# Differential attention: issuing the score matmuls of the two components in turn, each into its own bank

## The chip, the cores and the metric

The kernel runs as one program on one core of one Trainium2 chip. The metric is the device time of one execution in microseconds (us): 2513.7 us is the median of three runs of the kernel before (2513.29 to 2515.72). The engines go by their short names: PE is TensorE, DVE VectorE, ACT ScalarE, POOL GpSimd, SP SyncE with the DMA queue that it issues.

## The reference, cut to what matters

The program is two transformer blocks in float32 on 512 tokens of width 1024: a state space branch and a mixture of experts, then a recurrent layer (RWKV-7) and a layer of differential attention. The change lies in that attention, the last layer, where each of 8 heads has two components (c) of 64 dimensions:

```python
def block(args):                       # 128 queries at a time
    q_blk, blk = args
    s = jnp.einsum('bhcqd,bhckd->bhcqk', q_blk.astype(f32), kf)
    q_pos = blk * Q_BLOCK + jnp.arange(Q_BLOCK)
    s = jnp.where(k_pos[None, :] <= q_pos[:, None], s, -1e30)
    prob = jax.nn.softmax(s, axis=-1)
    attn = prob[:, :, 0] - lam * prob[:, :, 1]
    return jnp.einsum('bhqk,bhkv->bhqv', attn, vf)
```

The result is normalized over the 128 values of a head, multiplied by `silu(gate)` and projected.

## The kernel before, in words

A float32 product is made of three matmuls of a rounded kind (float32r): each operand is split into a high and a low part, and high by high, high by low and low by high are added up in one PSUM bank. `mm3` (L199 to L206) does it for the projections (L205), `hilo` (L222 to L224) splits: the high part on ACT (L223), the low part on DVE or POOL (L224).

`LayerB.run` (L2376) goes through 32 units, one for each head `m` and block of 128 queries `i`, for the heads 0 to 5 in the order i = 0, 1, 2, 3. A unit of block `i` has `n = 128 (i + 1)` keys, since the mask is causal. `unit` (L2280) is a generator of three steps:

- Step one, the score maps. For each component c, three matmuls at L2297 (64 partitions of k and q: 0 to 63 for c = 0, 64 to 127 for c = 1) fill a map of 128 x n in a PSUM tile `sm`. DVE adds the mask to its last 128 columns (L2298) and takes the maximum (L2299), ACT exponentiates with the sum of each row (L2300). Then DVE puts the two components together into one map `e0` (L2302 to L2304; L2304 is the large one).
- Step two. PE transposes `e0` block by block (L2309) into another `sm`, ACT copies it to `aT` (L2311), PE multiplies by the values into the bank `o` (L2313). ACT squares and sums (L2316), DVE (L2317) and POOL (L2318) make the factor, ACT writes the scaled `ot` (L2319).
- Step three, for odd `i`: PE transposes the `ot` of the two latest blocks into an `sm` (L2326), DVE multiplies by the gate into `y` (L2328), which is then split.

The tag `sm` has three PSUM banks (L2287), shared by all of this. A round of `run` takes step three of the unit before the last, step two of the last and step one of the new one.

Between the units stand steps of `head_in` (L2223), which projects k, q and gate of the next head: 24 matmuls at L205 for each of six groups, on PE alone. For k and q the partly rotated positions follow: ACT copies the result to `rp` (L2243), SP moves four bands of it to `turn` by DMA (L2246), POOL multiplies `rp` (L2248) and DVE multiplies `turn` (L2249) by tables of cosines and sines, DVE adds (L2250) and the sum is split into `hdkh`, `hdkl` or `hdqh`, `hdql`.

The order of instructions on each engine isn't that of the code. The program is recorded under a tile framework with `schedule_with_timeline_sim=True`: it keeps the data's dependences and picks the order by a timeline of its own, and `issue_after` (L2232) holds back the projections' matmuls until the marked score matmul of an earlier unit (`self.marks`, L2301). At run time each engine goes through its list in that order and waits at semaphores.

Of the kernel before, what the change touches and what calls it, by code (L numbers as in the profile page):

```python
# [1571 lines left out]
class Pre:  # L1572
# [25 lines left out]
    def t(self, n, b=1, w=512, dt=F32):  # L1598
        return self.sp.tile([P, w], dt, tag="p_" + n, name="p_" + n, bufs=b)
# [543 lines left out]
class LayerB:  # L2143
# [136 lines left out]
    def unit(self, m, i, hd, o, yo):  # L2280

        g, nc = self.g, self.g.nc
        t = lambda shape, name, bufs=2: self.sp.tile(shape, F32, tag=name, name=name, bufs=bufs)
        sm = lambda: g.ps.tile([P, 512], F32, tag="sm", name="sm", bufs=3)  # L2287
        kr, qr = hd["k"], hd["q"]
        n = (i + 1) * P
        qs = slice(i * P, n)  # L2290
        r, mx = t([P, 6], "sums", 4), t([P, 2], "mx")
        e = [t([P, 512], "e%d" % c) for c in range(2)]
        for c in range(2):
            f = slice(64 * c, 64 * c + 64)
            p = sm()
            for j, (a_, b_) in enumerate(((qr[0], kr[0]), (qr[0], kr[1]), (qr[1], kr[0]))):
                mark = nc.tensor.matmul(p[:, :n], lhsT=a_[f, qs], rhs=b_[f, :n], start=j == 0, stop=j == 2).ins  # L2297
            nc.vector.tensor_add(p[:, qs], p[:, qs], self.cst[:, 1024:])  # L2298
            nc.vector.tensor_reduce(mx[:, c:c + 1], p[:, :n], axis=AX.X, op=OP.max, negate=True)  # L2299
            nc.scalar.activation(e[c][:, :n], p[:, :n], AF.Exp, bias=mx[:, c:c + 1], accum_out=r[:, c:c + 1])  # L2300
        self.marks.append(mark)  # L2301
        nc.vector.reciprocal(r[:, 2:3], r[:, 1:2])  # L2302
        nc.vector.scalar_tensor_tensor(r[:, 2:3], r[:, 2:3], self.nlam, r[:, 0:1], op0=OP.mult, op1=OP.mult)
        nc.vector.scalar_tensor_tensor(e[0][:, :n], e[1][:, :n], r[:, 2:3], e[0][:, :n], op0=OP.mult, op1=OP.add)  # L2304
        nc.vector.scalar_tensor_tensor(r[:, 3:4], r[:, 0:1], 1e-5, r[:, 0:1], op0=OP.mult, op1=OP.mult)
        yield 1
        p = sm()
        for j in range(i + 1):
            nc.tensor.transpose(p[:, j * P:(j + 1) * P], e[0][:, j * P:(j + 1) * P], g.ident)  # L2309
        aT = t([P, 512], "aT")  # L2310
        nc.scalar.activation(aT[:, :n], p[:, :n], AF.Copy)  # L2311
        for j in range(i + 1):
            nc.tensor.matmul(o[:, qs], lhsT=aT[:, j * P:(j + 1) * P], rhs=self.vt[:, j, m * P:(m + 1) * P],  # L2313
                             start=j == 0, stop=j == i)
        ot = t([P, P], "ot", 4)
        nc.scalar.activation(ot, o[:, qs], AF.Square, accum_out=r[:, 4:5])  # L2316
        nc.vector.scalar_tensor_tensor(r[:, 4:5], r[:, 4:5], 1.0 / 128, r[:, 3:4], op0=OP.mult, op1=OP.add)  # L2317
        nc.gpsimd.tensor_tensor(r[:, 5:6], r[:, 4:5], g.mhalf[:, 0:1], op=OP.pow)  # L2318
        nc.scalar.activation(ot, o[:, qs], AF.Copy, scale=r[:, 5:6])  # L2319
        yield 1  # L2320
        th, d = divmod(i, 2)
        hd["o", i] = ot
        if d:
            p = sm()
            for c in range(2):
                nc.tensor.transpose(p[:, c * P:(c + 1) * P], hd["o", i - 1 + c], g.ident)  # L2326
            y = t([P, 256], "y")
            nc.vector.scalar_tensor_tensor(y, p[:, :256], self.sl, hd["g"][:, 256 * th:256 * th + 256], op0=OP.mult,  # L2328
                                           op1=OP.mult)
            g.hilo(yo[th][0][:, m], yo[th][1][:, m], y)  # L2330
# [141 lines left out]
```

## Time and profile before

| | |
|---|---|
| median of three runs | 2513.7 us |
| the profiled execution's own time | 2504.29 us |
| its span, first to last instruction | 2502.5 us |
| PE, DVE, ACT, POOL busy | 91%, 52%, 35%, 31% of the span |
| units of attention, first score map to the last unit's | 2173.5 to 2418 us of the span |

The time of a row in the timeline is counted from the start of the span. A matmul's end is modelled: one of 256 columns is shown with 0.28 us while the next starts 0.12 us after it, so what PE takes is read from starts. In the timeline equal instructions that follow each other in time stand in one row with their count (x2). "[1.16 <-DVE e L2304]" behind a row is the engine's idle time before it and what ended it. PEclk is the granted clock of TensorE: 1.00 is 2.4 GHz and 0.50 is 1.2 GHz.

### The profile page before, as it was taken

The numbers are of one execution on the slowest core, as the hardware profiler recorded it, in microseconds if no ns is written. First come the engines' busy times: TensorE is split into PE (matmuls) and PEld (weight loads), VectorE is DVE, ScalarE is ACT, GpSimd is POOL, SyncE is SP. The second block draws the span as 40 slices with busy tenths as digits, with TensorE's granted clock in tenths as the row PEclk, the third lists the DMA queues.
The fourth block names the chain that finished last, engine by engine and source line by source line (L and its number), as shares of the span: only waits on it lengthen the run. The fifth ranks groups of instructions, "written<-read, shape, count | busy, mean of one in ns | idle before, by whom it ended". The sixth has DMA issues, their size and how long they took to land. (4 is left out here: it accounts for less than half of the span.)

```text
span 2502.5 us, 31640 instructions
## 1 busy us (share of the span) xinstructions
PE 2283.3 (91%) x11912; PEld 1641.4 (66%) x11912; DVE 1308.8 (52%) x2382; ACT 876.6 (35%) x1597; POOL 771.3 (31%) x596
## 2 busy tenths in 40 slices
PE   6899999998998999999989976998979899999997
PEld 3677888776886544443334335666868798988887
DVE  5567877767643433211111126758525556477765
ACT  3443333343322211111111115535326644354552
POOL 2333434114001122222212224449324221655212
PEclk9899999999999999999999987999979999999998
DMA  7232333344733889999999963576765432122211
GB/s 287 94 101 101 103 108 108 119 145 159 268 101 119 338 302 399 381 347 387 399 382 362 376 203 117 152 187 189 205 175 200 144 105 88 56 60 65 79 65 51
DMA packets 187178, 477.16 MB, mean 191 GB/s; under 512 B 62333, under 2 KB 111869, under 8 KB 146832
## 3 DMA queue, kind: packets, MB, share of 16 engines
q1 hardware_dynamic: 161392, 424.48, 47.1%
q0 software_dynamic: 16288, 37.21, 5.7%
q10 hardware_dynamic: 9344, 13.44, 1.8%
q8 instruction: 94, 1.54, 0.2%
q14 instruction: 60, 0.49, 0.1%
HBM read 423.66 MB, written 71.89 MB: 198 GB/s over the span
## 5 line engine op out<-in xcount | busy, mean ns | idle before, releaser
L224 POOL TENSOR_TENSOR wl<-wr,wh 128x1024 fp32r<-128x1024 f32 x80 | 202.9, 2553 | 373.2 <-ACT wh L223 373.2
L223 ACT ACTIVATE wh<-wr 128x1024 fp32r<-128x1024 f32 (+1 forms) x202 | 204.3, 1043 | 236.1 <-PE mm L205 147.7
L205 PE MATMUL mm<-uh,wh 128*128 128x512 f32 x640 | 258.4, 404 | 10.4 <-DVE cv L604 7.6
L205 PE MATMUL mm<-ul,wh 128*128 128x512 f32 x640 | 256.1, 400 | 0.0
L205 PE MATMUL mm<-uh,wl 128*128 128x512 f32 x640 | 255.7, 400 | 0.0
L1196 PE MATMUL mm<-m_we,m_x 128*64 128x512 f32 (+1 forms) x672 | 250.7, 599 | 0.3 <-DMA m_we<-in_w_exp_dram 0.3
L205 PE MATMUL mm<-ya,wh 128*128 128x256 f32 x1280 | 243.9, 291 | 6.8 <-ACT wh L223 6.7
L205 PEld LDWEIGHTS mm<-ya,wh 128*128 128x128 f32 x1280 | 204.9, 196 | 13.9 <-ACT wh L223 7.9
L224 DVE TENSOR_TENSOR wl<-wr,wh 128x1024 fp32r<-128x1024 f32 (+1 forms) x122 | 154.7, 1286 | 65.6 <-ACT wh L223 65.3
L205 PE MATMUL mm<-ya,wl 128*128 128x256 f32 x640 | 184.6, 289 | 0.0
L1186 DVE COPY m_x<-sm 128x512 f32<-128x512 f32 x48 | 33.2, 691 | 289.5 <-PE mm L1196 226.5
L1196 PE MATMUL mm<-m_wl,m_x 128*64 128x512 f32 (+1 forms) x432 | 169.1, 601 | 5.9 <-DMA m_wl<-in_w_exp_dram 5.9
L1196 PEld LDWEIGHTS mm<-m_we,m_x 128*64 128x64 f32 (+1 forms) x672 | 86.8, 159 | 111.4 <-issue 108.8
L1196 PE MATMUL mm<-m_we,m_ht 128*64 128x512 f32 (+1 forms) x368 | 140.8, 601 | 11.4 <-ACT m_y L1236 6.7
L205 PEld LDWEIGHTS mm<-uh,wh 128*128 128x128 f32 x640 | 122.3, 191 | 41.5 <-issue 8.1
L205 PEld LDWEIGHTS mm<-ul,wh 128*128 128x128 f32 x640 | 122.0, 191 | 29.0 <-issue 0.3
L205 PEld LDWEIGHTS mm<-uh,wl 128*128 128x128 f32 x640 | 121.7, 190 | 29.3
L1169 POOL DMA_INDIRECT m_xg<-u_d,sgi x48 | 50.4, 1050 | 273.5 <-PE sm L1184 81.1
L205 PEld LDWEIGHTS mm<-ya,wl 128*128 128x128 f32 x640 | 125.3, 196 | 0.5
L1522 PE MATMUL mm<-xh,wh 128*128 128x512 f32 x256 | 106.3, 418 | 5.7 <-ACT xh L223 3.4
L1248 POOL DMA_INDIRECT rt_d<-m_y,sgi x46 | 70.9, 1542 | 125.0 <-ACT m_y L1236 35.2
L1522 PE MATMUL mm<-xl,wh 128*128 128x512 f32 x256 | 105.6, 413 | 4.0 <-DVE xl L224 2.8
(575 smaller groups left out, 4839.9 us busy)
## 6 DMA issues: line engine op xcount, KB each, us to landing
m_we<-in_w_exp_dram SPq DMA_DIRECT2D x117, 1024.0 KB
m_wl<-in_w_exp_dram SPq DMA_DIRECT2D x78, 1024.0 KB
wr<-in_w_grp_dram SPq DMA_DIRECT2D x32, 1024.0 KB
wr<-in_w_ada_dram SPq DMA_DIRECT2D x18, 1024.0 KB
ck<-pk_d SPq DMA_DIRECT2D x16, 1024.0 KB
csb<-cs_d ACTq DMA_DIRECT2D x16, 512.0 KB
wr<-in_w_pg_dram SPq DMA_DIRECT2D x8, 1024.0 KB
raw<-in_w_ada_dram SPq DMA_DIRECT2D x6, 1024.0 KB
```

The costliest lines, as they stand in the source:

```text
L205: nc.tensor.matmul(pt, lhsT=l, rhs=r, start=n == 0, stop=n == last)
L223: self.nc.scalar.activation(hi, src, AF.Copy)
L224: return (eng or self.nc.vector).tensor_sub(lo, src, hi.bitcast(F32)).ins
L1169: self.g.nc.gpsimd.indirect_dma_start(out=xg, out_offset=None, in_=self.u2_d, bounds_check=511, oob_is_err=False, in_offset=bass.IndirectO ...
L1186: nc.vector.tensor_copy(x[:, 4:], v_(p, 4))
L1196: self.mark = self.g.nc.tensor.matmul(p[s], lhsT=x[:, s], rhs=w, start=start, stop=stop).ins
L1248: nc.gpsimd.indirect_dma_start(out=self.rt_d[self.turn], out_offset=bass.IndirectOffsetOnAxis(ap=ix, axis=0), in_=y[:ix.shape[0]], in_offs ...
L1522: nc.tensor.matmul(p, lhsT=a_[:, s], rhs=b_, start=k == 0 and i == 0, stop=k == 7 and i == 2)
```

## The change

The two `sm` tiles of a unit are taken at the start, and the loops change places: the term (high by high, low by high, high by low) is now the outer loop and the component the inner one. The mask, the maximum and the exponential of both components come behind all six matmuls. What is computed stays the same, and so does the number of instructions on every engine. Below L2297 the line numbers grow by one (L2304 is L2305 afterwards, L2309 is L2310).

```diff
-        for c in range(2):
-            f = slice(64 * c, 64 * c + 64)
-            p = sm()
-            for j, (a_, b_) in enumerate(((qr[0], kr[0]), (qr[0], kr[1]), (qr[1], kr[0]))):
-                mark = nc.tensor.matmul(p[:, :n], lhsT=a_[f, qs], rhs=b_[f, :n], start=j == 0, stop=j == 2).ins
+        ps = [sm(), sm()]
+        for j, (a_, b_) in enumerate(((qr[0], kr[0]), (qr[0], kr[1]), (qr[1], kr[0]))):
+            for c in range(2):
+                f = slice(64 * c, 64 * c + 64)
+                mark = nc.tensor.matmul(ps[c][:, :n], lhsT=a_[f, qs], rhs=b_[f, :n], start=j == 0, stop=j == 2).ins
+        for c, p in enumerate(ps):
             nc.vector.tensor_add(p[:, qs], p[:, qs], self.cst[:, 1024:])
             nc.vector.tensor_reduce(mx[:, c:c + 1], p[:, :n], axis=AX.X, op=OP.max, negate=True)
```

Since a scheduler sets the order, other instructions move too. On PE, in head 1, block 2 (maps of 384 columns, `sm_16179` for component 0), the list before reads:

```order
L2309 MATMUL sm_16163<-cst_70,e0_16101 128x128 x2
L2297 MATMUL sm_16179<-hdkh_15769,hdqh_15869 128x384
L2297 MATMUL sm_16179<-hdkl_15770,hdqh_15869 128x384
L2297 MATMUL sm_16179<-hdkh_15769,hdql_15870 128x384
L2297 MATMUL sm_16186<-hdkh_15769,hdqh_15869 128x384
L2297 MATMUL sm_16186<-hdkl_15770,hdqh_15869 128x384
L2297 MATMUL sm_16186<-hdkh_15769,hdql_15870 128x384
```

and afterwards:

```order
L2310 MATMUL sm_16163<-cst_70,e0_16101 128x128 x2
L2297 MATMUL sm_16179<-hdkh_15769,hdqh_15869 128x384
L2297 MATMUL sm_16180<-hdkh_15769,hdqh_15869 128x384
L2297 MATMUL sm_16179<-hdkl_15770,hdqh_15869 128x384
L2297 MATMUL sm_16180<-hdkl_15770,hdqh_15869 128x384
L2297 MATMUL sm_16179<-hdkh_15769,hdql_15870 128x384
L2297 MATMUL sm_16180<-hdkh_15769,hdql_15870 128x384
```

Here the components now take turns. This is so in 17 of the 32 units; in the other 15 the three matmuls of a component still follow each other.

Among these 15 are the blocks 3 (maps of 512 columns). On PE in head 1, block 3, before (the projections' matmuls of L205 that follow are 17; `sm_16234` takes the transposed `ot`):

```order
L2309 MATMUL sm_16241<-cst_70,e0_16177 128x128 x3
L2297 MATMUL sm_16259<-hdkh_15769,hdqh_15869 128x512
L2297 MATMUL sm_16259<-hdkl_15770,hdqh_15869 128x512
L2297 MATMUL sm_16259<-hdkh_15769,hdql_15870 128x512
L2297 MATMUL sm_16266<-hdkh_15769,hdqh_15869 128x512
L2297 MATMUL sm_16266<-hdkl_15770,hdqh_15869 128x512
L2297 MATMUL sm_16266<-hdkh_15769,hdql_15870 128x512
L205 MATMUL mm_16481<-ya_12683,wh_16372 128x256
```

and afterwards:

```order
L2310 MATMUL sm_16241<-cst_70,e0_16177 128x128 x3
L2297 MATMUL sm_16259<-hdkh_15769,hdqh_15869 128x512
L2297 MATMUL sm_16259<-hdkl_15770,hdqh_15869 128x512
L2297 MATMUL sm_16259<-hdkh_15769,hdql_15870 128x512
L2327 MATMUL sm_16234<-cst_70,ot_16170 128x128
L2314 MATMUL o_15978<-vt_15153,aT_16245 128x128 x3
L2297 MATMUL sm_16260<-hdkh_15769,hdqh_15869 128x512
L2297 MATMUL sm_16260<-hdkl_15770,hdqh_15869 128x512
L2297 MATMUL sm_16260<-hdkh_15769,hdql_15870 128x512
L205 MATMUL mm_16481<-ya_12683,wh_16372 128x256
```

The transpose of `ot` and the product with the values, which stood behind 17 or 18 of the projections' matmuls, now stand between the two components, and all 24 projections' matmuls come behind them. This holds for block 3 of the heads 0 to 4.

On DVE at the same place, between the two maps of block 2 and those of block 3, the list before reads:

```order
L2299 TENSOR_REDUCE mx_16176<-sm_16186 128x1
L2305 SCALAR_TENSOR_TENSOR sums_16175<-sums_16175 128x1
L2302 RECIPROCAL sums_16175<-sums_16175 128x1
L2303 SCALAR_TENSOR_TENSOR sums_16175<-sums_16175,ls_15434 128x1
L2317 SCALAR_TENSOR_TENSOR sums_16099<-sums_16099 128x1
L2304 SCALAR_TENSOR_TENSOR e0_16177<-e1_16178,sums_16175,e0_16177 128x384
L2249 TENSOR_TENSOR turn0_15431<-turn0_15431,acst_15429 128x512
L2250 TENSOR_TENSOR rp_16425<-turn0_15431,rp_16425 128x512
```

and afterwards:

```order
L2300 TENSOR_REDUCE mx_16176<-sm_16180 128x1
L2306 SCALAR_TENSOR_TENSOR sums_16175<-sums_16175 128x1
L2303 RECIPROCAL sums_16175<-sums_16175 128x1
L2304 SCALAR_TENSOR_TENSOR sums_16175<-sums_16175,ls_15434 128x1
L2318 SCALAR_TENSOR_TENSOR sums_16099<-sums_16099 128x1
L2249 TENSOR_TENSOR turn0_15431<-turn0_15431,acst_15429 128x512
L2305 SCALAR_TENSOR_TENSOR e0_16177<-e1_16178,sums_16175,e0_16177 128x384
L2250 TENSOR_TENSOR rp_16425<-turn0_15431,rp_16425 128x512
```

The multiplication of `turn` (L2249) has moved ahead of the map `e0`, in the heads 0 to 4.

## Rows read from the trace of the kernel before

**Rows 1.** The page: busy time of each engine (share of the span) x instructions.

```profile
PE 2283.3 (91%) x11912; PEld 1641.4 (66%) x11912; DVE 1308.8 (52%) x2382; ACT 876.6 (35%) x1597; POOL 771.3 (31%) x596
```

**Rows 2.** Windows, the attention's units: from:to, length, busy (count) by engine, PEclk, DMA.

```profile
2173.50:2421.00 247.50, 230.72 (x1732) 210.73 (x1733) 173.43 (x400) 128.30 (x361) 96.31 (x86) 0.97 0.21 64
```

**Rows 3.** Waits of PE, 2173.5 to 2425 us: us in total, times, longest.

```profile
PE sm L2309 <- DVE e L2304: 12.9, 12, 2.5
```

**Rows 4.** Timeline of PE, head 1, block 2: start, length, what, count.

```profile
2225.50 0.45 PE L2297 MATMUL sm<-hdkh,hdqh 64*128 64x384 f32 x2
2225.78 0.34 PE L2297 MATMUL sm<-hdkl,hdqh 64*128 64x384 f32 x2
2225.95 0.34 PE L2297 MATMUL sm<-hdkh,hdql 64*128 64x384 f32 x2
```

**Rows 5.** Timeline of PE, head 1, block 3.

```profile
2231.08 0.52 PE L2309 MATMUL sm<-cst,e 128*128 128x128 f32 x3 [1.16 <-DVE e L2304]
2231.53 0.50 PE L2297 MATMUL sm<-hdkh,hdqh 64*128 64x512 f32 x1
...
2232.18 0.49 PE L2297 MATMUL sm<-hdkh,hdqh 64*128 64x512 f32 x1
...
2233.06 0.51 PE L205 MATMUL mm<-ya,wh 128*128 128x256 f32 x2
...
2235.21 0.27 PE L2326 MATMUL sm<-cst,ot 128*128 128x128 f32 x1
...
2235.90 0.36 PE L205 MATMUL mm<-ya,wl 128*128 128x256 f32 x1
...
2237.53 0.63 PE L2309 MATMUL sm<-cst,e 128*128 128x128 f32 x4 [0.55 <-DVE e L2304]
```

**Rows 6.** Timeline of PE, transposes before and after block 3, heads 0, 2, 3, 4.

```profile
2199.91 0.52 PE L2309 MATMUL sm<-cst,e 128*128 128x128 f32 x3 [2.51 <-DVE e L2304]
...
2209.62 0.63 PE L2309 MATMUL sm<-cst,e 128*128 128x128 f32 x4 [1.05 <-ACT wh L223]
...
2260.11 0.52 PE L2309 MATMUL sm<-cst,e 128*128 128x128 f32 x3 [2.29 <-DVE e L2304]
...
2269.21 0.63 PE L2309 MATMUL sm<-cst,e 128*128 128x128 f32 x4 [1.72 <-DVE e L2304]
...
2290.68 0.52 PE L2309 MATMUL sm<-cst,e 128*128 128x128 f32 x3 [1.16 <-DVE e L2304]
...
2298.34 0.63 PE L2309 MATMUL sm<-cst,e 128*128 128x128 f32 x4 [0.29 <-DVE e L2304]
...
2319.98 0.52 PE L2309 MATMUL sm<-cst,e 128*128 128x128 f32 x3 [1.16 <-DVE e L2304]
...
2326.48 0.63 PE L2309 MATMUL sm<-cst,e 128*128 128x128 f32 x4 [0.61 <-DVE e L2304]
```

**Rows 7.** Timeline of DVE, POOL and ACT, head 1, ahead of block 3.

```profile
2230.32 0.61 DVE L2304 SCALAR_TENSOR_TENSOR e<-e,sums,e 128x384 f32<-128x384 f32 x1
2230.90 0.69 DVE L2249 TENSOR_TENSOR turn<-turn,acst 128x512 f32<-128x512 f32 x1
...
2231.09 1.65 POOL L2248 TENSOR_TENSOR rp<-rp,acst 128x512 f32<-128x512 f32 x1 [6.75 <-DMA turn<-rp]
...
2233.28 0.37 ACT L2319 ACTIVATE ot<-o,sums 128x128 f32<-128x128 f32 x1 [1.16 <-POOL sums L2318]
```

**Rows 8.** Timeline of DVE and POOL, head 0, the same place.

```profile
2198.40 1.36 DVE L2304 SCALAR_TENSOR_TENSOR e<-e,sums,e 128x384 f32<-128x384 f32 x1
2199.68 1.75 DVE L2249 TENSOR_TENSOR turn<-turn,acst 128x512 f32<-128x512 f32 x1
...
2199.30 1.58 POOL L2248 TENSOR_TENSOR rp<-rp,acst 128x512 f32<-128x512 f32 x1
```

**Rows 9.** Timeline of DVE, head 1, block 3: the second map's mask.

```profile
2234.32 0.29 DVE L2298 TENSOR_TENSOR sm<-sm,acst 128x128 f32<-128x128 f32 x1
```

**Rows 10.** Windows, head 3, block 3: a stretch at the lower clock.

```profile
2292.60:2296.00 3.40, 3.40 (x16) 3.30 (x16) 2.60 (x6) 2.47 (x6) 1.63 (x2) 0.50 0.01 2
```

## The prediction

> **What bounds the kernel now.** I read the busy shares first: PE is busy 91% of the span [rows 1]. Then the attention, the only stage that the change touches: in 247.5 us PE is busy 230.7 us, DVE 173.4 us, at a mean granted clock of 0.97 [rows 2]. So PE sets the pace there too, and what it waits for is to be looked up: its largest wait by far is the transposes at L2309 for the map `e0` that DVE writes at L2304, 12.9 us in 12 waits [rows 3]. Last I read the timeline of PE around these waits. The five blocks 3 of the heads 0 to 4 all have one ahead of them (2.51, 1.16, 2.29, 1.16, 1.16 us), and all have one behind them, before the transposes of four blocks (1.05, 0.55, 1.72, 0.29, 0.61 us) [rows 5, 6]. Everywhere else the projections' matmuls cover the softmax. So the question is twofold: do the score matmuls themselves get shorter, and what does the new order do to these five places?
>
> **The change part by part.**
>
> *The components in turn, 17 units.* Nothing is gained here, I take it. The list of before has all three matmuls of component 0 ahead of those of component 1, but the trace shows them in pairs: two starts of the first term at 2225.50, two of the second from 2225.78, two of the third from 2225.95 [rows 4]. The halves of the array are filled by both components at once already. The check is the pace: 17 projections of 256 columns fill the 2.15 us from 2233.06 to 2235.21, 0.12 us each and a little for the change to full height [rows 5], so 384 columns take 0.18; with six in a row the fifth would start 0.72 us after the first, and here the last pair starts 0.45 us after it. Of the 17 units that now alternate, 8 are blocks 0, 8 blocks 2 and one a block 1; the rows of the others read the same way. Value taken: 0. If the pairs were serial today and became parallel, each unit would save three matmuls: 8 x 0.18 + 1 x 0.36 + 8 x 0.54 = 6.1 us.
>
> The Trainium skill speaks for that saving: "TensorE: Matmul & The Clock Gate", part 3, "The mechanism", says that matmuls start and end strictly in program order. By that rule the six of before would stand one behind the other, and the change would be worth 6.1 us. The rows 4 don't agree: the second component's first matmul starts ahead of two that precede it in the list.
>
> *The blocks 1.* Their two maps stood apart before, with projections and a product between them, and stand apart after, with about as many. No cost.
>
> *The blocks 3 of five heads, first step: `e0` comes later.* The list of DVE now puts L2249 ahead of the map `e0` for which PE waits. That is more than its 0.69 us, since POOL's L2248 gets ready at the same moment (both wait for the DMA of `turn`), and the two engines hold each other up. Head 0 shows it: POOL multiplies from 2199.30 to 2200.88, and the L2249 that DVE starts at 2199.68 takes 1.75 us in place of 0.69 and ends 0.55 us after POOL; the map `e0` ahead of it took 1.36 us in place of 0.61 [rows 7, 8]. So the three run one after another in any order, and `e0` was the first of them and becomes the last. In head 1 it ended at 2230.93; afterwards L2249, then L2248 (until 2231.09 + 1.65 = 2232.74), then `e0`, 0.55 us later at 2233.29: 2.36 us late. I take the same for heads 3 and 4, whose waits before were the same 1.16 us. In head 0 the third of the three ended at 2201.43 and `e0` at 2199.76: 1.67 us late; the same for head 2. Sum: 3 x 2.36 + 2 x 1.67 = 10.4 us. PE has nothing else in its list between the blocks' products and these transposes, so all of it is idle time. The bound from below: `e0` isn't held by POOL and follows L2249 at once, 2231.59 + 0.61, or 1.27 us late, and 0.69 in heads 0 and 2: 5.2 us.
>
> *Second step: from the transposes of three blocks to those of four.* Before, this took 9.71, 6.45, 9.10, 7.66 and 6.50 us, 39.4 in all [rows 5, 6]. Afterwards PE does, in this order: transposes (0.45 until the first map), the first map alone (0.88, as the second takes from 2232.18 to 2233.06), the transpose of `ot` and the product (0.69, from 2235.21 to 2235.90), the second map (0.88), 24 projections (24 x 0.12 = 2.9): 5.8 us, and 5.9 with the added change between half and full height [rows 5]. Waiting for `ot` costs nothing further: ACT ends it at 2233.65 [rows 7], and the first map, itself late, is done later: `e0` at 2233.29, 0.15 us until the transposes as before (2230.93 to 2231.08), 0.45 and 0.88 make 2234.8. But the last transposes want the second map's softmax. From its mask at 2234.32 to them at 2237.53 it was 3.2 us [rows 5, 9]; now the mask can start some 3.4 us after the transposes (the second map is done at 3.0, and DVE has the first one's work ahead). That makes 6.6 us, more than PE's 5.9, so `e0` decides again, at about what head 1 took (6.45). The projections that used to stand in front of `ot` covered a wait that no longer exists, and can't help the one behind.
>
> *The clock.* In head 3 the granted clock lay at 0.50, the lower level, from 2292.6 to 2296.0 [rows 10], after an idle time of 1.16 us and the sparse work around it; the block took 7.66 us against 6.45, 1.2 us more. After the idle times of 2.29 and 2.51 us heads 2 and 0 were slow as well; heads 1 and 4, with 1.16 us, weren't. The idle times become 3.5 us (heads 1, 3, 4) and 4.0 to 4.2 us, so I expect the lower clock in all five: 5 x (6.6 + 1.2) = 39.0 us, 0.4 less than now. Bounds: no spell at all gives 5 x 6.6 = 33.0, 6.4 less than now; spells as costly as head 0's give 5 x 9.71 = 48.6, 9.1 more.
>
> *Nothing catches up.* From the transposes of four blocks to the next block 2, PE goes from one matmul to the next, with the same number of projections in both lists; a delay at block 3 stays to the end.
>
> **Sum.** 0 + 10.4 - 0.4 = 10.0 us, or 2504.3 + 10.0 = 2514.3 us for the profiled execution. The median of the runs lies 9.4 us above that execution; I add the same 10.0 to it: 2523.7 us.
>
> **The rivals.**
>
> *Faster: the pairs were serial after all and now overlap.* Place: the 17 alternating units; price 6.1 us, 2507.6 us if the blocks 3 also came out even. It decides the result from the point where the third pair starts more than 0.72 us after the first in the trace of before and less afterwards. Against it stand the rows 4. I give it 0.06.
>
> *No change: the late `e0` is paid for by what it removes.* `e0` follows L2249 directly (5.2 us), and the lower clock is absent (6.4 us less): 2512.5 us; with `e0` held by POOL and no low clock, 10.4 - 6.4 = 4.0, 2517.7 us. For it: the clock's spells fell on only three of the five heads. Against: they came where PE idled longest, and it will idle longer. 0.24.
>
> *Slower by twice as much: long stretches at half clock.* Each block 3 costs head 0's 9.71 us: 10.4 + 9.1 = 19.5, 2533.2 us. For it: PE's work between idle time and projections becomes sparser, since the maps no longer overlap. Against: a single head did so. 0.12.
>
> *The forecast*, around 10 us slower: 0.58.
>
> **How the numbers follow.** A run can tell 0.2%, or 5 us, from no change. Slower by more than that: the forecast, the long stretches, less 0.01 for the forecast's lower edge: 0.69. Within: 0.25. Faster: 0.06. The range goes from 2513 (`e0` only just late, low clock gone) to 2533 (long stretches in every head); below it lie the faster rival and the edge of "no change", above it what exceeds head 0's spell, some 0.15 together.
>
> **What would show it.** Right: in the trace afterwards PE waits for `e0` before block 3 of heads 0 to 4 for 3.5 to 4.2 us where 1.16 to 2.51 stood, DVE's `e0` map there ends about 0.55 us after POOL's L2248, and the steps inside alternating units stay as they are. Wrong: the waits before the transposes of three blocks grow by 0.7 us or less (POOL doesn't hold DVE); the third pair of a block 2 starts clearly less than 0.45 us after the first (there was something left to overlap); or the projections behind block 3 run at the full clock throughout.

## The result, and the profile after

The changed kernel takes 2536.8 us (median of 5 runs, 2530.9 to 2538.2) where the kernel before, run beside it, takes 2513.3 (median of 5, 2504.3 to 2515.7): a ratio of 1.0101, with a 95% interval of 1.0085 to 1.0116. It is slower, as forecast, but by some 24 us instead of 10, and outside the range. The profiled execution took 2531.8 us, its span is 2530.0 us; that of before took 2504.3.

PE's busy time on the page of the kernel afterwards [rows 1]:

```profile
PE 2301.3 (91%) x11912; PEld 1652.7 (65%) x11912; DVE 1309.0 (52%) x2382; ACT 874.9 (35%) x1597; POOL 772.1 (31%) x596
```

The number of instructions is the same and PE is busy 18 us longer: part of the loss is slower work, not waiting. The window over the attention, of about the length of [rows 2], shows which:

```profile
2176.30:2424.30 248.00, 224.82 (x1597) 201.67 (x1598) 158.43 (x356) 114.18 (x323) 94.59 (x84) 0.93 0.20 64
```

In the same time PE gets 1597 matmuls done where it did 1732, and its mean granted clock is 0.93 where it was 0.97. What it waits for in the attention (in total, times, longest), against 12.9 us of [rows 3]:

```profile
PE sm L2310 <- DVE e L2305: 18.1, 7, 3.8
PE sm L2327 <- ACT ot L2320: 4.3, 7, 2.0
PE o L2314 <- ACT aT L2312: 1.8, 5, 0.4
```

The waits for `e0` are fewer and longer, and five each for `ot` and `aT`, one in every block 1, are new (the one wait of before for `ot`, 1.9 us ahead of the last score maps, is there in both, and head 0's block 3 has one of 0.5).

To see where the time went, I cut each head into three steps by the starts of PE's transposes of `e0`: T2 (two blocks), T3 (three), T4 (four), and T2 of the next head. Sums over the heads 0 to 4, in us, from PE's timeline in each profile (the kernels e1 to e12 are the experiments below; the medians of before lie between 2507.9 and 2513.3 us, so each ratio is to the runs of before that were taken beside the kernel):

| kernel | T2 to T3 | T3 to T4 | T4 to next T2 | sum | median us | ratio to before, interval |
|---|---|---|---|---|---|---|
| before | 31.9 | 39.4 | 78.1 | 149.4 | 2513.3 | |
| after | 40.5 | 46.6 | 84.1 | 171.2 | 2536.8 | 1.0101, 1.0085 to 1.0116 |
| e1 L2249 held | 31.5 | 37.3 | 80.1 | 148.9 | 2511.9 | 1.0000, 0.9984 to 1.0017 |
| e2 L2249 first, no turns | 42.5 | 47.2 | 82.2 | 171.9 | 2537.7 | 1.0104, 1.0077 to 1.0131 |
| e3 turns undone | 41.6 | 46.8 | 84.1 | 172.5 | 2537.9 | 1.0107, 1.0080 to 1.0135 |
| e4 turns alone | 31.9 | 39.4 | 78.1 | 149.4 | 2509.0 | 0.9994, 0.9977 to 1.0010 |
| e5 idle time filled | 41.1 | 38.4 | 80.2 | 159.8 | 2521.2 | 1.0062, 1.0046 to 1.0078 |
| e6 one pair on DVE | 31.6 | 52.0 | 84.1 | 167.6 | 2530.2 | 1.0093, 1.0073 to 1.0113 |
| e7 one pair on ACT | 41.0 | 50.9 | 82.8 | 174.8 | 2541.3 | 1.0135, 1.0119 to 1.0152 |
| e8 before, filled | 31.4 | 34.2 | 78.6 | 144.2 | 2507.6 | 0.9995, 0.9984 to 1.0007 |
| e9 `ot` made early | 41.5 | 50.0 | 79.3 | 170.7 | 2535.4 | 1.0101, 1.0085 to 1.0117 |
| e10 `wl` moved | 31.5 | 39.0 | 80.3 | 150.7 | 2511.1 | 1.0004, 0.9992 to 1.0015 |
| e11 before again | 32.1 | 38.4 | 77.9 | 148.4 | 2508.8 | 0.9997, 0.9986 to 1.0008 |
| e12 `e0` first | 26.5 | 40.9 | 80.9 | 148.3 | 2508.0 | 0.9992, 0.9978 to 1.0006 |

So the change costs 8.6 us from T2 to T3, 7.1 from T3 to T4 and 6.0 from T4 on: 21.7 of the 27.5 us by which the span of the profiled execution grew (the medians lie 23.5 us apart). Another 2.8 us lie ahead of the attention, where nothing was changed (its first score map starts at 2173.5 us before and 2176.3 afterwards; in the profiles of the experiments between 2175.0 and 2183.0). Behind the five heads it is 0.4 up to the last score maps and 2.6 from there to the end; e1 has the latter too (87.3 us, where before has 84.6), though it is as fast as before.

PE's timeline in head 1, block 2 (start, length, what, count), which answers [rows 4]:

```profile
2230.30 0.44 PE L2297 MATMUL sm<-hdkh,hdqh 64*128 64x384 f32 x2
2230.58 0.34 PE L2297 MATMUL sm<-hdkl,hdqh 64*128 64x384 f32 x2
2230.76 0.34 PE L2297 MATMUL sm<-hdkh,hdql 64*128 64x384 f32 x2
```

The starts lie 0.28 and 0.46 us behind the first; before it was 0.28 and 0.45. The alternation changes nothing here.

The same timeline at block 3, answering [rows 5]:

```profile
2238.09 0.52 PE L2310 MATMUL sm<-cst,e 128*128 128x128 f32 x3 [3.37 <-DVE e L2305]
2238.54 0.50 PE L2297 MATMUL sm<-hdkh,hdqh 64*128 64x512 f32 x1
...
2239.43 0.42 PE L2327 MATMUL sm<-cst,ot 128*128 128x128 f32 x1
2239.65 1.50 PE L2314 MATMUL o<-vt,aT 128*128 128x128 f32 x6
2241.07 0.79 PE L2297 MATMUL sm<-hdkh,hdqh 64*128 64x512 f32 x1
...
2242.65 0.79 PE L205 MATMUL mm<-ya,wh 128*128 128x256 f32 x2
...
2246.53 0.40 PE L205 MATMUL mm<-ya,wh 128*128 128x256 f32 x2
...
2247.24 0.60 PE L2310 MATMUL sm<-cst,e 128*128 128x128 f32 x4
```

T3 waits 3.37 us where it waited 1.16. From there to T4 PE doesn't wait at all, and yet needs 9.15 us. The first map takes 0.89 us, but the second 1.58 (2241.07 to 2242.65), and the projections up to 2246.01 start 0.21 us apart (the first two 0.38) where those from 2246.53 start 0.12 apart. Windows from T3 to T4 of heads 1 and 4 afterwards (busy by engine, then the granted clock):

```profile
2238.09:2247.24 9.15, 9.15 (x40) 7.59 (x41) 5.34 (x12) 3.87 (x11) 2.10 (x3) 0.63 0.00 0
2340.76:2349.87 9.11, 9.11 (x40) 7.47 (x41) 4.61 (x12) 3.87 (x11) 2.10 (x3) 0.63 0.07 31
```

and the same heads before:

```profile
2231.07:2237.52 6.45, 5.90 (x40) 4.97 (x41) 4.96 (x12) 4.15 (x11) 3.45 (x3) 1.00 0.00 0
2319.98:2326.48 6.50, 5.89 (x41) 4.96 (x41) 4.98 (x12) 4.22 (x11) 3.51 (x3) 1.00 0.40 147
```

The mean granted clock falls from 1.00 to 0.63, and the same forty matmuls keep PE busy for 9.1 us instead of 5.9. In the clock's records each of the five heads has a stretch of 6.8 us at 0.50, the lower level of 1.2 GHz; before, three heads had one, of 6.8, 3.4 and 3.4 us.

Why `e0` is late is seen on DVE, and on POOL, which answer [rows 7]:

```profile
2235.05 0.16 DVE L2318 SCALAR_TENSOR_TENSOR sums<-sums 128x1 f32<-128x1 f32 x1
2235.72 0.69 DVE L2249 TENSOR_TENSOR turn<-turn,acst 128x512 f32<-128x512 f32 x1 [0.50 <-DMA turn<-rp]
2236.32 1.62 DVE L2305 SCALAR_TENSOR_TENSOR e<-e,sums,e 128x384 f32<-128x384 f32 x1
```

```profile
2235.90 1.62 POOL L2248 TENSOR_TENSOR rp<-rp,acst 128x512 f32<-128x512 f32 x1 [6.12 <-DMA turn<-rp]
```

DVE stands at L2249 for the DMA of `turn`, while `e0` could run; then L2248 has begun, and `e0` takes 1.62 us in place of 0.61 and ends 0.42 us after it. Head 0 differs: there `e0` (2201.40 to 2202.79) still goes ahead of L2248 (from 2202.34 on) and ends 0.42 us after another multiplication on POOL, L2178.

Last, the new waits at block 1 of the next head. On PE:

```profile
2256.45 0.33 PE L2327 MATMUL sm<-cst,ot 128*128 128x128 f32 x1 [0.34 <-ACT ot L2320]
2257.14 0.49 PE L2314 MATMUL o<-vt,aT 128*128 128x128 f32 x2 [0.36 <-ACT aT L2312]
```

and on ACT, afterwards:

```profile
2247.32 1.06 ACT L223 ACTIVATE wh<-wr 128x1024 fp32r<-128x1024 f32 x1 [2.73 <-PE mm L205]
...
2256.03 0.37 ACT L2320 ACTIVATE ot<-o,sums 128x128 f32<-128x128 f32 x1 [3.70 <-POOL sums L2319]
2256.30 0.62 ACT L223 ACTIVATE hdqh<-rp 128x512 fp32r<-128x512 f32 x1
2256.81 0.27 ACT L2312 ACTIVATE aT<-sm 128x128 f32<-128x128 f32 x1
```

and before:

```profile
2236.90 1.06 ACT L223 ACTIVATE wh<-wr 128x1024 fp32r<-128x1024 f32 x1 [0.18 <-PE mm L205]
...
2245.62 0.37 ACT L2319 ACTIVATE ot<-o,sums 128x128 f32<-128x128 f32 x1 [2.49 <-POOL sums L2318]
```

From the rounding of `wh`, which PE's last projections of block 3 release, to the end of `ot` it takes 9.1 us in both (2236.90 to 2245.99, 2247.32 to 2256.40); on the way lie the DMA of `turn`, L2249 and POOL's L2248. PE's way from T4 to the transpose of this `ot` is 8.8 us. Before, PE waited 0.55 us at T4 [rows 5], and so `ot` was there 0.3 us ahead of PE. Afterwards PE waits nothing at T4 and comes too early here.

### The profile page after: what moved, and what is told of

It is laid out like the page before. It is cut to its first block, busy times and chain, and to the rows that moved or that the text cites. A ratio compares the mean times of both kernels' runs of the same rounds, so it can differ in the third digit from the quotient of the medians.

```text
span 2530.0 us, 31634 instructions
## 1 busy us (share of the span) xinstructions
PE 2301.3 (91%) x11912; PEld 1652.7 (65%) x11912; DVE 1309.0 (52%) x2382; ACT 874.9 (35%) x1597; POOL 772.1 (31%) x596
## 5 line engine op out<-in xcount | busy, mean ns | idle before, releaser
L224 POOL TENSOR_TENSOR wl<-wr,wh 128x1024 fp32r<-128x1024 f32 x80 | 203.1, 2555 | 374.2 <-ACT wh L223 374.2
L205 PE MATMUL mm<-uh,wh 128*128 128x512 f32 x640 | 259.2, 406 | 9.5 <-DVE cv L604 7.3
L205 PE MATMUL mm<-ul,wh 128*128 128x512 f32 x640 | 257.0, 402 | 0.0
L205 PE MATMUL mm<-uh,wl 128*128 128x512 f32 x640 | 256.1, 400 | 0.0
L205 PE MATMUL mm<-ya,wh 128*128 128x256 f32 x1280 | 246.9, 294 | 6.7 <-ACT wh L223 6.7
L205 PEld LDWEIGHTS mm<-ya,wh 128*128 128x128 f32 x1280 | 207.8, 199 | 15.8 <-ACT wh L223 8.4
L224 DVE TENSOR_TENSOR wl<-wr,wh 128x1024 fp32r<-128x1024 f32 (+1 forms) x122 | 154.6, 1284 | 92.1 <-ACT wh L223 89.3
L205 PE MATMUL mm<-ya,wl 128*128 128x256 f32 x640 | 185.5, 290 | 0.0
L1196 PE MATMUL mm<-m_we,m_ht 128*64 128x512 f32 (+1 forms) x368 | 140.8, 601 | 11.4 <-ACT m_y L1236 6.7
L205 PEld LDWEIGHTS mm<-uh,wh 128*128 128x128 f32 x640 | 122.7, 192 | 40.9 <-issue 7.7
L205 PEld LDWEIGHTS mm<-uh,wl 128*128 128x128 f32 x640 | 122.3, 191 | 29.5
L205 PEld LDWEIGHTS mm<-ul,wh 128*128 128x128 f32 x640 | 122.4, 191 | 28.9 <-issue 0.3
L205 PEld LDWEIGHTS mm<-ya,wl 128*128 128x128 f32 x640 | 127.0, 199 | 0.1
```

The lines of the kernel that those rows point to most:

```text
L205: nc.tensor.matmul(pt, lhsT=l, rhs=r, start=n == 0, stop=n == last)
L224: return (eng or self.nc.vector).tensor_sub(lo, src, hi.bitcast(F32)).ins
L1196: self.mark = self.g.nc.tensor.matmul(p[s], lhsT=x[:, s], rhs=w, start=start, stop=stop).ins
```

## The experiments

In e1 and e2 one queue order is given to the scheduler, which then arranges the rest. In the others that change an order, the order of every engine is written down as found and fixed, and only the rows named are moved.

**e1: L2249 held behind `e0`, the components still in turn.** (The lines that note each `e0` aren't shown.)

```diff
-                nc.vector.tensor_mul(r, r, sinT)
+                with g.tc.issue_after(self.e0[m - 2, 2]) if n == "k" and m > 1 else contextlib.nullcontext():
+                    nc.vector.tensor_mul(r, r, sinT)
```

> The changed kernel, with one thing put back: on DVE the multiplication of turn (L2249) of head m+2's k is queued behind the map e0 of head m, block 2. The maps of the blocks 0 and 2 still alternate between the components. Theory 'order' (the 24 us come from e0 being the last of three that exclude each other, and from what the scheduler builds on that): the time goes back to that of before, 2513 +- 5 us; PE's waits ahead of the transposes of three blocks are 1.2 to 2.5 us again, and those transposes to those of four take 6.5 to 9.7 us with the lower clock in at most three heads. Rival 'alternation' (the turns themselves cost PE time or hold back the first component's softmax): it stays near 2537 us. Rival 'hidden gain' (the turns save something that the order eats): below 2508 us.

Measured: 2511.9 us, a ratio of 1.0000 (0.9984 to 1.0017) to before. The waits of PE for `e0` in the attention are those of before again:

```profile
PE sm L2311 <- DVE e L2306: 12.6, 11, 2.2
```

T3 to T4 takes 8.75, 6.55, 7.78, 6.55 and 7.66 us. One order edge gives everything back, to within the interval, with the turns in all 17 units in place. On PE the block 3 of head 1 has its two maps one after the other again, with `ot`'s transpose behind them.

**e2: the counterpart, `e0` held behind L2249 in the kernel before.** (The lines that note `e0` and L2249 and define `no` aren't shown.)

```diff
+        for m in range(5):
+            self.g.tc.add_manual_dep(self.e0[m, 2], self.tm[m + 2, "k"].name, no, reason="late")
```

> The kernel before, the components one behind the other as they were, with one thing taken from the change: on DVE the map e0 of block 2, heads 0 to 4, is queued behind L2249 (k of the head after the next). Theory 'order': 2535 +- 5 us, with waits of 2.8 to 3.8 us ahead of the transposes of three blocks, 9.1 us from them to those of four in all five heads and the granted clock at 0.50 for 6.8 us in each. Rival 'alternation': 2513 +- 5 us. If only the delay of e0 counts and the clock spells came from the alternation: 2522 us.

Measured: 2537.7 us, 1.0104 (1.0077 to 1.0131), the changed kernel's time without its change. The waits for `e0`:

```profile
PE sm L2309 <- DVE e L2304: 20.3, 8, 4.2
```

T3 waits 3.4 to 4.2 us in each head, T3 to T4 takes 8.3 to 10.6 us, and the scheduler, given this one pair, also puts the transpose of `ot` and the product between the maps of block 3. No run moves this pair alone in the fixed lists of the kernel before, so what the late `e0` costs without the scheduler's other moves isn't shown.

**e3 and e4: the alternation by itself.** e3 takes the turns out of nine of the changed kernel's 17 alternating units (the blocks 2 and a block 1; the blocks 0 keep theirs). e4 puts turns into twelve units of the kernel before (blocks 2 and 3 and a block 1, none of the blocks 0). On the other engines no row moves.

```diff
 e4, PE, head 1, block 2
 A: hdkh,hdqh
+B: hdkh,hdqh
 A: hdkl,hdqh
+B: hdkl,hdqh
 A: hdkh,hdql
-B: hdkh,hdqh
-B: hdkl,hdqh
 B: hdkh,hdql
```

> The changed kernel with every engine's list as it is, but on PE the six score matmuls of the blocks 2 (and of head 0's block 1), which alternated, are put back to three of component 0 and then three of component 1: nine units. Theory 'order': same time as the changed kernel, 2537 +- 4 us, and the two first terms of a unit still start within 0.05 us of each other. Rival 'alternation': about half of the loss comes back, some 2525 us. Rival 'hidden gain', where alternating saves three matmuls of 0.18 us in each unit: 4.9 us slower than the changed kernel, 2542 us.

> The kernel before with every engine's list as it is, but on PE the six score matmuls of the blocks 2 and 3 of heads 0 to 4 (one block 1 and one block 2 of head 5 too, and where the six stand together) are put in turns: component 0 and 1 of the first term, of the second, of the third. This is what the change is in words, and nothing else moves. Theory 'order': 2513 +- 4 us, no change. Rival 'alternation': slower by 5 us or more. Rival 'hidden gain': 12 units save 0.54 to 0.72 us each, so some 2506 us.

Measured: e3 2537.9 us, no different from the changed kernel; e4 2509.0 us, 0.9994 (0.9977 to 1.0010), no different from before. e4's three steps agree with those of before to 0.1 us, and its block 2 starts its terms as before:

```profile
2231.20 0.44 PE L2323 MATMUL sm<-hdkh,hdqh 64*128 64x384 f32 x2
2231.48 0.33 PE L2323 MATMUL sm<-hdkl,hdqh 64*128 64x384 f32 x2
2231.65 0.34 PE L2323 MATMUL sm<-hdkh,hdql 64*128 64x384 f32 x2
```

So what the change is in words costs and gains nothing that the runs can tell; for the blocks 0 that rests on e1 alone, which keeps all 17 turns and takes the time of before. What the change does to the scheduler's order is the whole difference.

**e5: PE's idle time ahead of T3 filled, nothing else.** Ten matmuls per head write a bank that the transposes then overwrite (only the added matmuls are shown). They fill the wait but for 1.0 to 1.4 us.

```diff
         p = sm()
+        fill = [nc.tensor.matmul(p[:, :512], lhsT=qr[0][:, :P], rhs=kr[0][:, :512], start=True, stop=True).ins
+                for j in range(10 if i == 2 and m < 5 else 0)]
         for j in range(i + 1):
```

> The changed kernel with every engine's list kept as it is, and ten matmuls of 512 columns more on PE ahead of the transposes of three blocks, heads 0 to 4. Their results are overwritten by these transposes; they only fill the 2.8 to 3.8 us in which PE waits for e0. Theory 'idle time' (the wait ahead is what drops the granted clock to 0.50 for 6.8 us, and that is why the next step takes 9.1 us): the clock stays up in these heads, the transposes of three blocks to those of four take 6 to 7 us, 5 x 2.5 = 12.5 us or more come back, and with a wait at the transposes of four some of the block 1's 6 us too: 2519 to 2525 us, though 50 matmuls were added. Rival 'sparse work' (the single maps, the transpose of ot and the product behind the transposes, with no components side by side, are what drops the clock): the step stays at 9.1 us, 2537 us or a little more.

Measured: 2521.2 us, 1.0062 (1.0046 to 1.0078) where the changed kernel has 1.0101 (1.0085 to 1.0116): 50 more matmuls make it 0.39% or 10 us faster, and the five heads 11.4 us shorter in the profile. T3 to T4 in heads 0, 1 and 3:

```profile
2202.54:2211.69 9.15, 9.14 (x40) 7.49 (x41) 6.52 (x12) 3.61 (x10) 6.45 (x7) 0.63 0.01 2
2236.70:2243.21 6.51, 6.32 (x40) 5.03 (x41) 4.48 (x12) 3.89 (x12) 2.23 (x3) 1.00 0.00 0
2300.03:2307.25 7.22, 6.32 (x41) 5.03 (x41) 4.58 (x12) 4.79 (x13) 2.17 (x3) 1.00 0.01 3
```

`e0` is as late as before the filling (T2 to T3 41.1 us), but in four of five heads the clock stays at 1.00 and PE waits at T4 again. In these heads the block 1 also recovers as far as PE waits at T4: with a wait of 0.20 us T4 to the next T2 takes 16.35 us, with 0.90 to 2.00 us 15.6 to 15.7; in head 0, with none, 16.97.

In four of five heads the idle time is thus what drops the clock. Its length alone doesn't decide: head 0 keeps its stretch with 1.39 us of waiting left, head 2 loses it with 1.41. The Trainium skill, too, names idle time: "TensorE: Matmul & The Clock Gate", part 1, "HAM oscillation", tells that a long wait between bursts of matmuls throttles PE again, so that the next burst starts slow. The trace agrees in these four heads: a granted clock of 0.63 without the filling and of 1.00 with it.

**e6: only the pair on DVE put back.**

```diff
 DVE, heads 0 to 4, block 2
+L2305 e0<-e1,sums,e0
 L2249 turn0<-turn0,acst
-L2305 e0<-e1,sums,e0
```

> The changed kernel with every engine's list kept as it is except one pair on DVE in heads 0 to 4: e0 of block 2 stands ahead of L2249 again. PE still has the transpose of ot and the product between the two maps of block 3. Theory 'order' in parts: the waits ahead of the transposes of three blocks go back to 1.2 to 2.5 us (8.6 us less); the clock spells get shorter or vanish in some heads (3 to 7 us less); block 1 keeps its waits for ot and aT (up to 6 us). Together 2519 to 2525 us. Rival 'the rest of the list' (PE's new place for ot's transpose and the product is what costs): 2528 us or more. If the pair is everything: 2513 us, as with L2249 held in the scheduler.

Measured: 2530.2 us, 1.0093 (1.0073 to 1.0113); the rival's number, and by the ratio hardly different from the changed kernel. The waits ahead of T3 do go back to 1.16 to 2.25 us. But PE's list still has `ot`'s transpose between the two maps, and now PE gets there before `ot` (with the fixed order written into its file the lines count higher; L2381 is L2310):

```profile
2242.42 0.52 PE L2381 MATMUL sm<-cst,e 128*128 128x128 f32 x3 [1.16 <-DVE e L2376]
...
2243.43 0.39 PE L2368 MATMUL sm<-hdkh,hdql 64*128 64x512 f32 x1
2245.04 0.33 PE L2398 MATMUL sm<-cst,ot 128*128 128x128 f32 x1 [1.22 <-ACT ot L2391]
```

T3 to T4 grows to 52.0 us, again at a low clock. So the places on PE fit a late `e0`, and only e1, where the scheduler rearranges both, is as fast as before.

**e7 and e9: the waits at block 1.** e7 moves `aT` on ACT; e9 also takes `ot`'s chain out from behind the DMA of `turn`.

```diff
 ACT, block 1 (e7, e9)
+L2312 aT<-sm
 L223 hdqh<-rp
-L2312 aT<-sm
 DVE (e9)
+L2318 sums<-sums
 L2249 turn0<-turn0,acst
-L2318 sums<-sums
 POOL (e9)
+L2319 sums<-sums,mhalf
 L2248 rp<-rp,acst
-L2319 sums<-sums,mhalf
```

> The changed kernel with every engine's list kept as it is except one pair on ACT in five heads: in block 1 the copy aT (L2312) goes ahead of the rounding of hdqh (L223), as before the change. Theory: PE's wait of 0.36 us for aT goes, and the product starts some 0.5 us earlier: 5 x 0.5 = 2.5 us less than the changed kernel, 2534.5 us; the wait of 0.34 us for ot stays, since ot comes at the end of a chain through the DMA of turn that nothing here shortens. Rival (the aT order is the whole loss of block 1): 6 us less, 2531 us. Rival (hidden by the wait for ot): no change, 2537 us.

> The changed kernel with every engine's list kept as it is except three pairs in five heads, around block 1: on DVE L2318 (the sum for ot of block 3) goes ahead of L2249, on POOL its power L2319 goes ahead of L2248, and on ACT aT goes ahead of the rounding of hdqh. So ot of block 3 no longer stands behind the DMA of turn. Theory 'the wait is paid later' (block 1's 6 us are this chain, from the last projection of block 3 over the DMA of turn to ot, which was covered before by PE's wait ahead of the transposes of four blocks): in the profile both waits of block 1 (0.34 us for ot, 0.36 us for aT) vanish, and from the transposes of four blocks to the next head's transposes of two it takes 15.6 us in place of 16.7 to 17.0, so 6 us less than the changed kernel, if the clock's spells stay where they are. Rival (PE's own order there costs the 6 us): 16.7 us or more, no change. What the clock does with it is open: where aT alone was moved, the spells grew.

Measured: e9 removes both waits, and T4 to the next T2 comes down to 15.5 or 15.6 us in heads 1, 3 and 4, and to 16.3 in 0 and 2, where PE now waits 0.6 us for the next `e0`: 79.3 in all, 4.8 less. That confirms the chain in the profile. But e9 takes 2535.4 us, no less than the changed kernel, and e7 2541.3, even more (1.0135, 1.0119 to 1.0152, against 1.0101, 1.0085 to 1.0116), where 2531 to 2537 us were expected. In both T3 to T4 grew, to 50.0 and 50.9 us, since the stretches at the lower clock became longer (47.8 us in the five heads of each, where the changed kernel has 34.1). The window over the five heads in e7:

```profile
2201.19:2375.94 174.75, 154.35 (x1010) 135.92 (x1011) 113.76 (x240) 73.85 (x210) 71.93 (x64) 0.86 0.18 56
```

PE is busy 154 us at a clock of 0.86. Why a wait taken away there lengthens the low stretch 16 us on, at waits ahead of T3 that changed in one head of each alone (e7: 4.33 us for 3.80 in head 2; e9: 3.74 for 2.76 in head 0), no run tells; it stays open. The stretches add up to 37.6 us in e3 already, which waits for `e0` as the changed kernel does but for head 0 (3.80 us for 2.76).

**e8 and e11: the filling in the kernel before, and that kernel once more.** The edit is that of e5, with eight matmuls in heads 0 and 2 and four in 1, 3 and 4.

> The kernel before with every engine's list kept as it is, and matmuls of 512 columns more on PE ahead of the transposes of three blocks: eight in heads 0 and 2, four in heads 1, 3 and 4, overwritten by the transposes. Theory 'idle time': the spells at the lower clock in heads 0, 2 and 3 vanish, the steps of 9.71, 9.10 and 7.66 us come down to 6.5, and the kernel gets 6.8 us faster than before, 2505 us where before is 2512; this would beat both. Rival 'sparse work': no change, 2512 us. Rival: the added matmuls hold back the transposes, 2514 us or more.

> The kernel before, unchanged, for a second profile on the same chip as the others of this call. If its steps in the attention are the same as in the first profile (waits of 2.51, 1.16, 2.29, 1.16, 1.16 us; 9.71, 6.45, 9.10, 7.66, 6.50 us), the spells at the lower clock belong to the kernel and not to the run, and what differs from run to run lies ahead of the attention. If they move, the 5 us that the added matmuls took out of the attention of before, without a faster median, would be such a difference.

Measured: e8 2507.6 us, 0.9995 (0.9984 to 1.0007); e11 2508.8. In e8 no stretch at the lower clock is left in the five heads:

```profile
2201.51:2345.67 144.16, 137.92 (x1039) 124.10 (x1040) 112.34 (x240) 74.76 (x210) 74.87 (x64) 1.00 0.22 69
```

and in e11:

```profile
2198.53:2346.92 148.39, 135.27 (x1011) 122.79 (x1012) 109.58 (x240) 74.88 (x210) 72.33 (x64) 0.97 0.21 67
```

The 4.2 us show in the profile and not in the medians. e11 has the steps of before to 0.15 us but for head 3, whose 7.66 us became 6.54 without a stretch there, so a part of the spells belongs to the run. A gain of up to 0.16% can't be excluded; shown it is not.

**e10 and e12: the chain to `e0` shortened in the kernel before.** e10 moves `wl` (L224, 1.22 us) out of block 2's chain on DVE, behind L2249. e12 puts `e0` ahead of `wl` and L2317, and L2249 and L2250 behind the masks and maxima of block 3; on ACT the rounding of `hdkh` goes behind the two exponentials of block 3.

```diff
 e12, DVE, heads 0 to 4, block 2 and on
-L224 wl<-wr,wh
 ...
 L2303 sums
+L2304 e0<-e1,sums,e0
+L224 wl<-wr,wh
 L2317 sums<-sums
-L2304 e0<-e1,sums,e0
-L2249 turn0, L2250 rp
 L2298, L2299 (both components of block 3)
+L2249 turn0, L2250 rp
```

> The kernel before with every engine's list kept as it is except one instruction on DVE in heads 0 to 4: the rounding wl (L224, 1.22 us), which stands between the mask and the maximum of block 2's first component, goes behind L2249. So the map e0 of block 2, which PE waits for, comes about 1.1 us sooner. Theory (what the change lost is this chain from block 2's maps to e0; then the same chain made shorter must gain): waits ahead of the transposes of three blocks of 0 to 0.2 us in heads 1, 3, 4 and about 1.3 us in heads 0 and 2, 5.5 us less, and fewer or shorter spells at the lower clock, up to 5 us less: 2501 to 2506 us where before is 2511; faster than both kernels. Rival: wl comes too late for the projections, and PE waits for it instead: no change or slower.

> The kernel before, lists kept on PE and POOL, with the chain to e0 rearranged in heads 0 to 4. On DVE e0 of block 2 goes ahead of L2317 (which waits for PE's own product by way of ACT, and behind which e0 stood 1.1 us in the run with wl alone moved); wl (L224) and L2317 follow it; L2249 and L2250 go behind the masks and maxima of block 3; on ACT the rounding of hdkh goes behind the two exponentials of block 3. Corrected theory (the wait ahead of the transposes of three blocks is e0 queued behind L2317): these waits fall from 1.16 us to 0.2 or less in heads 1, 3, 4 and to about 1.4 us in heads 0 and 2; transposes of three to those of four 6.0 to 6.5 us; no or few spells at the lower clock; the waits at block 1 stay away as long as PE still waits ahead of the transposes of four. In all 8 to 12 us less than before: 2498 to 2503 us where before is 2510, faster than both kernels. Rival (POOL's L2248 holds DVE in any order): e0 as late as before, no change.

Measured: e10 2511.1 us, 1.0004 (0.9992 to 1.0015), my theory failed: T3 still waits 1.16 or 1.17 us in heads 1, 3 and 4. Its DVE shows why (the lines count 72 higher here; L2389 is L2317, L2376 is `e0`):

```profile
2236.86 0.22 DVE L2375 SCALAR_TENSOR_TENSOR sums<-sums,ls 128x1 f32<-128x1 f32 x1
2238.15 0.16 DVE L2389 SCALAR_TENSOR_TENSOR sums<-sums 128x1 f32<-128x1 f32 x1 [1.07 <-ACT ot L2388]
2238.22 0.61 DVE L2376 SCALAR_TENSOR_TENSOR e<-e,sums,e 128x384 f32<-128x384 f32 x1
```

`e0` is ready at 2237.1 and stands behind L2317, which waits by way of ACT for PE's own product. e12 mends that: in head 1, T3 starts 0.06 us behind the end of the transpose of `ot` (2236.67):

```profile
2236.40 0.27 PE L2398 MATMUL sm<-cst,ot 128*128 128x128 f32 x1
2236.73 0.52 PE L2381 MATMUL sm<-cst,e 128*128 128x128 f32 x3
...
2244.30 0.63 PE L2381 MATMUL sm<-cst,e 128*128 128x128 f32 x4 [1.68 <-ACT rp L2315]
```

But T4 now waits 1.68 us. The row names ACT's `rp`; the map `e0` of block 3 ended at 2244.16, 0.14 us ahead, as usual. It was held by POOL's rounding of `hdkl`, which waits for the `hdkh` that e12 moved back, as DVE and POOL show:

```profile
2238.51 0.69 DVE L2371 TENSOR_REDUCE mx<-sm 128x1 f32<-128x512 f32 x1
...
2239.44 0.69 DVE L2371 TENSOR_REDUCE mx<-sm 128x1 f32<-128x512 f32 x1
...
2242.36 1.80 DVE L2376 SCALAR_TENSOR_TENSOR e<-e,sums,e 128x512 f32<-128x512 f32 x1
```

```profile
2237.85 1.28 POOL L2320 TENSOR_TENSOR rp<-rp,acst 128x512 f32<-128x512 f32 x1 [6.74 <-ACT aT L2383]
...
2242.33 1.28 POOL L224 TENSOR_TENSOR hdkl<-rp,hdkh 128x512 fp32r<-128x512 f32 x1 [2.70 <-ACT hdkh L223]
```

From T2 to T4 it takes 12.35 us in head 1, as in the kernel before (12.34). The 8 to 12 us expected didn't come: 2508.0 us, 0.9992 (0.9978 to 1.0006). No version tried is measurably faster than the kernel before.

## Why the prediction was right and wrong

*The components in turn, 17 units: 0.* Right; e3 and e4 show it from both sides, and e1 for all 17 units.

*First step, `e0` comes later: 10.4 us.* Right in place, and in mechanism but for head 0; 8.6 us measured. The heads 1, 3 and 4 came at 2.2 to 2.3 us each, as worked out (2.36), with waits of 3.37 to 3.46 us; head 2 came at 1.5 where I had 1.67, and head 0 at 0.2. In head 0 I had misread the rows: its `e0` ends 0.41 us after POOL's L2178 in the kernel before (which ends at 2199.35) and 0.42 us after it in the changed one, so it didn't become the last of the three. e1 and e2 show that this pair decides, though e6 shows that it doesn't act alone.

*Second step and the clock: -0.4 us.* This is the step that failed; it measured +7.1. I let the second map's softmax end the step, at 6.6 us, and gave the low clock 1.2 us a head, which was head 3's price with a stretch of 3.4 us. In fact the stretch lasts 6.8 us in every head, PE's own work grows from 5.9 to 9.1 us, and the last transposes no longer wait for `e0` at all. The upper bound that I had worked out from head 0, 48.6 us for the five, was nearly reached (46.6). e5 shows the cause: with the idle time filled, the step falls to 38.4 us, and in the four heads at the full clock the second map's softmax decides again, as I had it, at 6.5 to 8.3 us. The traces of before had the hint: its two longest waits, 2.51 and 2.29 us, went with the two slowest steps, and I expected waits of 3.5 us and more but priced them by the mildest case.

*The blocks 1 and "nothing catches up": 0.* Failed too, +6.0 us; it is this that took the time out of the range, as 2536.8 less 6.0 is 2530.8 (an estimate, as if the rest stayed as it is). I compared the number of matmuls between the transposes, which is indeed the same, and overlooked that PE's wait at T4 was the slack of the next chain. When it vanished, that chain, through the DMA of `turn`, became the bound. e9 shows it by removing both waits (4.8 us less in these steps, though not in the median), e5 by bringing the slack back.

*The rivals.* "Slower by twice as much", with long stretches at half clock in each head, was the right picture of the second step, and its 2533.2 us lay nearest, in part by luck: it had 10.4 + 9.1 us, and nothing for the blocks 1. I gave it 0.12. In the profiled execution the sum is 8.6 + 7.1 + 6.0 us in the five heads; of the 2.6 us behind the last maps I can't say what they cost, since e1 has them too.

## What to carry to other kernels

Where a scheduler sets the order, a change is first of all another order: fix the lists and move one pair to see which part counts. A wait that goes away is also slack that goes away, so ask which chain on another engine was hidden by it. And an idle time on PE is priced with the slow stretch behind it, by the longest one that the trace shows and not by the mildest.

## What the runs showed of the hardware

Matmuls that compute nothing of use can pay for themselves: ten of them in each of five waits took 10 us out of the changed kernel; in four of five heads the granted clock stayed at 1.00 from T3 to T4 where it had been 0.63. In the kernel before a like filling brought nothing that the medians show (e8).

POOL doesn't hold all of DVE's instructions alike. `e0`, which reads two maps from SBUF, took 1.62 and 1.80 us beside POOL's L2248 and L224 in place of 0.61 and 0.75, while the maximum of block 3, which reads the score map in PSUM, took 0.69 us in e12 both beside POOL's L2248 (L2320 there, 2237.85 to 2239.13) and after it. The Trainium skill, "SBUF — State Buffer", "SBUF: two separate sides", says that a DVE operation with two SBUF inputs and a GpSimd operation that reads SBUF exclude each other for the whole instruction; the trace agrees, with `e0` ending 0.42 and 0.55 us after POOL's.
